# Expert mixture on one core: one row per token that experts gather, add to and scatter back, in place of three slots and a gather per group

## The chip, the cores and the metric

The kernel runs on one core of a Trainium2 chip. The metric is device time in microseconds of one execution; lower is better.

## What is computed

A trunk layer with two parts. The first mixes tokens: 2048 tokens and 16 meta tokens of width 1024 are normalised, projected by `w_in`, run through gated linear attention and latent attention, and projected back by `w_out`. The second is a hierarchical mixture of experts: a token chooses one of 8 groups and in it 2 of 8 experts; each expert is a SwiGLU of width 512. The sum of the residual row and the two weighted expert outputs is normalised at the end.

```python
h = h + concat([y_gla, y_mla]) @ w_out
t = rmsnorm(h, ffn_norm)
g_p, g_idx = top_k(softmax(t @ wg + bg), 1)                 # one of 8 groups
e_p, e_idx = top_k(softmax(e_logits_of_group), 2)           # two of its 8 experts
gates = g_p * e_p / sum(e_p)
ys = (silu(xb @ w_gate[e]) * (xb @ w_up[e])) @ w_down[e]    # per expert, its tokens
h = h + scatter_add(ys * gate)
out = rmsnorm(h, final_norm)[16:]
```

## The kernel before, in words

The program is recorded by a scheduling framework. Tiles are taken from pools with a number of buffers; the framework sets the order of the earlier phases on each engine, and the expert phase follows an order that a planner (`moe_plan`, L1475) works out from costs and due times. Every operation of the expert phase is recorded through one helper, so in the trace they all stand at L124 and are told apart by their tiles.

**Start.** `phase_z` (L149) loads tiles of x by SP (`load_x`, L162, DMA at L164), squares them on ACT (L170), normalises them on DVE (L173), and loads `w_in` in twelve pieces `wraw` of 128 x 1024 by ACT's queue (`load_w`, L177, DMA at L179). Each piece is split into two parts that a matmul in fp32r takes: `wh`, a cast on ACT (L182), and `wl`, a subtraction on DVE (L183). Every matmul of full precision is thus three.

**Rows in DRAM.** `out_proj` (L1157) writes the residual rows h into slot 0 of `yd`, a DRAM tensor of 2048 rows of 3 x 1024 floats (L1170), and the normalised rows into `ud`. Slots 1 and 2 are zeroed by `clear` (called at L985, defined at L993, DMA at L995): 32 writes of 512 KB on SP's queue. They depend on nothing but a small tile of zeros.

**Routing.** `route` (L1006), `odds` (L1080) and `weights` (L1100) work out group, experts, ranks and gates per pair of token tiles, and build tables: `src`, the token in each of 112 places of each expert's block, gate and scale columns of `tab`, and `gtab`, the tokens of each group, in up to 384 places.

**Experts.** `phase_moe` (L1598) runs one block of 112 places per expert, experts 0 to 63 in their order. Weights come in raw pieces of 1 MB, three per expert (`Weight`, L1348, SP's queue, 5 buffers `raw`), which ACT casts to `hi` and DVE subtracts to `lo`; of the down projection a half is used raw. The steps of a block, by the planner's names: GA gathers the block's rows of `ud` into `xs` (POOL, an indirect DMA); TX, XH, XL turn and split them; M_g and M_u are the gate and up matmuls into `pg`; SILU is on ACT; PROD on DVE (`h<-pg,tab,sg`); TH, HH, HL, HC turn and split `h`; M_d are the down matmuls into `pd`; Y multiplies `pd` by the gate on ACT (`weigh`, L1674, two halves of 112x512); SC scatters `y` into slot 1 or 2 of its token in `yd` (L1688, POOL).

After each eight experts, a group is complete. GF (`collect`, L1698) gathers its rows, three tiles `fo` of 128 rows of 12 KB, from `yd` by the table `g_dst`; A adds the three slots on DVE (L1702); SQ squares with a sum on ACT (L1707); RS and R take a logarithm and an exponential for the root (L1712), with loads of activation tables; L scales on DVE (`finish`, L1719); OD scatters the finished rows to the output (L1722, POOL). These steps lie among those of the next group's blocks; those of the last group come after the last matmul. Experts or groups with more tokens than places are handled behind the loop by code that does not run with these inputs.

Of the kernel before, what the change touches and what calls it, by code (L numbers as in the profile page):

```python
# [8 lines left out]
F32 = mybir.dt.float32  # L9
F32R = mybir.dt.float32r  # L10
# [39 lines left out]
YB = 3  # L50
# [25 lines left out]
def build(tc, a, dbg=None, stop=99):  # L76
    nc = tc.nc
    dbg = dbg or {}
    with ExitStack() as top:
# [7 lines left out]
        yd = dram.tile([SEQ, 3, D], F32, name="yd")  # L87
# [12 lines left out]
        env = dict(tc=tc, nc=nc, a=a, dbg=dbg, zf=zf, zv=zv, qd=qd, qrd=qrd, hg=hg, ud=ud, yd=yd, xlist=xlist, xexp=xexp,  # L100
# [657 lines left out]
def phase_mix(tc, nc, a, qd, qrd, hg, ud, yd, xlist, xexp, kv, ident, ones, eps, rt, keep, ctx, right, g_rest, g_close, **_):  # L758
# [10 lines left out]
    gpos = keep.tile([P, NT], F32, name="gpos")  # L769
    rt.update(gix=gix_, gpos=gpos, iob=iob, ids=ids, rank=rank, gates=gates, eix=eix, rstd=rstd)  # L770
    with ExitStack() as out:
# [196 lines left out]
        def finish(H):  # L968
# [15 lines left out]
            if H.h % 2:  # L984
                clear(2 * H.i + H.h // 2)  # L985
# [4 lines left out]
        zero = keep.tile([P, 1, D // 8], F32, name="zero")  # L990
        nc.gpsimd.memset(zero, 0.0)
# [14 lines left out]
        def route(lg, j):  # L1006
# [17 lines left out]
            nc.gpsimd.tensor_copy(Es[:, :, NE:], goh)  # L1024
            nc.vector.tensor_mul(Es[:, :, :NE].rearrange("p t (g j) -> p t g j", j=8), ohs[:, :, None, :].to_broadcast([P, 2, 8, 8]), gohb)
# [24 lines left out]
            for k in range(2):  # L1050
                nc.vector.tensor_mul(pr[:, k], E[:, k], ps[:, :, :NE])
# [28 lines left out]
        def odds(v, goh, oh, el, ps, js):  # L1080
# [12 lines left out]
            prg = O.so.tile([P, 2, 8], F32, name="prg", bufs=1)  # L1093
            nc.vector.tensor_mul(prg, goh, ps[:, :, NE:])
            gp1 = gpos[:, js]
            nc.vector.tensor_reduce(gp1, prg, axis=AX.X, op=OP.add)
            nc.vector.tensor_scalar_add(gp1, gp1, 1.0)
            return gd, e2

        def weights(gd, e2, goh, oh, E, R, js, last):  # L1100
            gp1 = gpos[:, js]
# [8 lines left out]
            yield  # L1110
            R2 = O.so.tile([P, 2, 2, BS], F32, name="R2", bufs=1)
            nc.scalar.copy(R2, R)
            V2 = O.so.tile([P, 2, 2, 2, NE], F32, name="V2", bufs=1)
            for k in range(2):
                for c, q in ((1, rstd[:, js]), (0, gates[:, k, js])):
                    (nc.vector if last else nc.gpsimd).tensor_mul(V2[:, k, :, c], E[:, k], q[:, :, None].to_broadcast([P, 2, NE]))
            yield
            pool, tag = O.w0 if last else O.w
            pb = pool.tile([BS, 2, NE], F32, name="ptab", tag=tag)
            for k in range(2):  # L1120
                for t in range(2):
                    nc.tensor.matmul(pb, R2[:, k, t], V2[:, k, t], start=k + t == 0, stop=k + t == 2)
            nc.vector.tensor_add(tab[:, 2:4], tab[:, 2:4], pb)
            yield
            V = O.so.tile([P, 2, 3, 8], BF16, name="Vg", bufs=1)
            for c in range(2):
                nc.vector.tensor_mul(V[:, :, c], goh, tv[:, c, js, None].to_broadcast([P, 2, 8]))
            nc.vector.tensor_copy(V[:, :, 2], goh)
            pool, tag = O.h0 if last else O.w
            gt = pool.tile([24, GB], F32, name="gt", tag=tag)  # L1130
            for t in range(2):
                R = O.so.tile([P, GB], BF16, name="Rg", tag="Rg", bufs=1)
                nc.vector.tensor_scalar(R, it, gp1[:, t:t + 1], None, op0=OP.is_equal)
                nc.tensor.matmul(gt, V[:, t].rearrange("p c g -> p (c g)"), R, start=t == 0, stop=t == 1)
            nc.vector.tensor_add(gtab, gtab, gt)
            yield
            w8 = O.so.tile([P, 3, 2, 8], F32, name="w8", bufs=1)
            i8 = O.iota8.to_broadcast([P, 2, 8])
            nc.gpsimd.tensor_mul(w8[:, 2], goh, i8)
            for k in range(2):  # L1140
                nc.gpsimd.tensor_mul(w8[:, k], oh[:, k], i8)
            ix = O.so.tile([P, 3, 2], F32, name="ix", bufs=1)
            nc.vector.tensor_reduce(ix, w8, axis=AX.X, op=OP.add)
            nc.gpsimd.tensor_copy(gix_[:, js], ix[:, 2])
            for k in range(2):
                nc.vector.scalar_tensor_tensor(eix[:, k, js], ix[:, 2], 8.0, ix[:, k], op0=OP.mult, op1=OP.add)
# [10 lines left out]
        def out_proj(i, xs, yh, yl, hs, t, hf):  # L1157
# [11 lines left out]
            if hf and hs[-1] == 3:  # L1169
                nc.sync.dma_start(yd[j * P:j * P + P, 0], x)  # L1170
# [208 lines left out]
def extra_blocks(nc, sp, ps, rt, ones, fl, xlist, xexp):  # L1379
# [12 lines left out]
    nc.gpsimd.iota(lim, pattern=[[BS, NXE]], base=0, channel_multiplier=0, allow_small_or_imprecise_dtypes=True)  # L1392
# [25 lines left out]
    nc.gpsimd.iota(xo, pattern=[[0, 2]], base=0, channel_multiplier=BS, allow_small_or_imprecise_dtypes=True)  # L1418
# [15 lines left out]
def make_index(nc, sp, tab, src, first, rows, n):  # L1434
    s = sp.tile([rows, n], F32, name="mi_s", tag="mi_s", bufs=1)
    nc.vector.tensor_scalar(s, tab, float(SEQ), -float(SEQ), op0=OP.is_ge, op1=OP.mult)
    nc.vector.tensor_add(src, s, tab)
    nc.vector.tensor_scalar(first, tab, float(SEQ), None, op0=OP.is_lt)


def slot_index(nc, sp, dix, src, first, rows, n):
    s = sp.tile([rows, n], F32, name="si_s", tag="si_s", bufs=1)
    nc.vector.tensor_scalar(s, src, 3.0, 2.0, op0=OP.mult, op1=OP.add)
    nc.vector.tensor_sub(dix, s, first)


def group_table(nc, sp, ps, p_t, rt, ident):
# [13 lines left out]
    yield  # L1461
    gT = p_t.tile([P, GT, 24], F32, name="gT", tag="t")
    for c in range(GT):
        nc.tensor.transpose(gT[:, c], rt["gtab"][:, c * P:c * P + P], ident[:24, :24])
    tok = sp.tile([P, GT, 8], F32, name="g_tok", bufs=1)
    nc.vector.tensor_scalar(tok, gT[:, :, 16:24], -float(FAR), float(FAR), op0=OP.mult, op1=OP.add)
    for c in range(2):
        nc.vector.tensor_add(tok, tok, gT[:, :, 8 * c:8 * c + 8])
    nc.vector.tensor_scalar_mul(fg, fl, float(FAR))
    dst = sp.tile([P, GT, 8], I32, name="g_dst", bufs=1)  # L1470
    nc.vector.tensor_tensor(dst, tok, fg[:, None, :].to_broadcast([P, GT, 8]), op=OP.add)
    rt.update(fl=fl, goh=goh, dst=dst)
# [463 lines left out]
```

## Time and profile before

| | us |
|---|---|
| median of 3 runs | 2576.59 (2574.45 to 2579.51) |
| the profiled execution | 2573.4 |
| its span in the trace | 2571.7 |
| PE busy in the span | 2384.5 (93%) |
| DVE busy | 1703.2 (66%) |
| ACT busy | 1363.4 (53%) |
| POOL busy | 517.2 (20%) |

The span is cut into stages by time. Busy times of an engine overlap those of the others. The DMA share is the mean busy share of the core's 16 DMA engines, PEclk the clock that was granted to PE, as a part of full speed. A bracket at the end of a line of the timeline says how long the engine stood idle before the instruction and what released it.

### The profile page before, as it was taken

Reading aid. Unit: us, or ns where it says so; the run is one execution under the profiler, and the core shown is the slowest. Engines: PE = TensorE matmul, PEld = TensorE weight load, DVE = VectorE, ACT = ScalarE, POOL = GpSimd, SP = SyncE. Lnnn points to the kernel's source line nnn. Section 1 sums busy time; section 2 is a strip of 40 time slices with the busy share of each in tenths; the row PEclk is TensorE's granted clock in tenths of the full one; section 3 lists DMA queues with packets and bytes.
Section 4 is the critical chain, followed back from the end, with each engine's and each line's share of the span. In section 5 each row is a group of like instructions: output and inputs, shape, how many; then the busy total and the mean of one; then the engine's idle time right before and its main releaser. Section 6 shows DMA issues by size and latency. Waiting matters only on the chain. (4 is left out here: it accounts for less than half of the span.)

```text
span 2571.7 us, 35285 instructions
## 1 busy us (share of the span) xinstructions
PE 2384.5 (93%) x12900; PEld 1892.3 (74%) x12900; DVE 1703.2 (66%) x2684; ACT 1363.4 (53%) x2101; POOL 517.2 (20%) x550
## 2 busy tenths in 40 slices
PE   3899999799999999999699989999999999999993
PEld 3799999678788989989567656666666667667662
DVE  2534243577667676777777767777777777777773
ACT  2312111555346555555366666675766767766672
POOL 0000000542000111212421223222122322223221
PEclk7899999899999999999799999999999999999997
DMA  9512112555331221220699999999999999999993
GB/s 307 187 53 78 62 52 85 161 188 173 131 130 46 77 80 63 69 72 34 242 323 377 370 338 364 375 372 376 366 378 379 373 368 375 370 364 378 368 375 132
DMA packets 184959, 605.19 MB, mean 235 GB/s; under 512 B 28172, under 2 KB 103452, under 8 KB 133580
## 3 DMA queue, kind: packets, MB, share of 16 engines
q1 hardware_dynamic: 158892, 526.49, 56.2%
q0 software_dynamic: 23440, 67.68, 7.1%
q10 hardware_dynamic: 2448, 8.72, 1.0%
q8 instruction: 103, 1.69, 0.3%
q14 instruction: 76, 0.62, 0.1%
HBM read 538.10 MB, written 106.63 MB: 251 GB/s over the span
## 5 line engine op out<-in xcount | busy, mean ns | idle before, releaser
L124 DVE TENSOR_TENSOR lo<-raw,hi 128x2048 fp32r<-128x2048 f32 x317 | 719.9, 2287 | 196.3 <-ACT hi L124 191.9
L124 ACT CAST hi<-raw 128x2048 fp32r<-128x2048 f32 x318 | 605.9, 1908 | 374.0 <-DMA raw<-in_w_gate_dram 207.9
L124 PE MATMUL pg<-hi,xh 128*112 128x512 f32 x1024 | 436.7, 426 | 0.9 <-ACT xh L124 0.9
L124 PE MATMUL pg<-lo,xh 128*112 128x512 f32 x1024 | 405.3, 396 | 16.7 <-DVE lo L124 16.7
L124 PE MATMUL pg<-hi,xl 128*112 128x512 f32 x1024 | 411.0, 401 | 9.2 <-DVE xl L124 9.2
L135 PE MATMUL ps<-uh,wh 128*128 128x256 f32 (+2 forms) x768 | 223.8, 292 | 31.9 <-ACT wh L182 20.8
L124 PEld LDWEIGHTS pg<-lo,xh 128*112 128x112 f32 x1024 | 181.6, 177 | 89.0 <-DVE lo L124 19.9
L124 PEld LDWEIGHTS pg<-hi,xl 128*112 128x112 f32 x1024 | 180.4, 176 | 72.1 <-DVE xl L124 13.3
L124 PEld LDWEIGHTS pg<-hi,xh 128*112 128x112 f32 x1024 | 180.3, 176 | 68.7 <-issue 9.6
L124 PE MATMUL pd<-raw,hc 128*112 128x512 f32 x512 | 230.1, 592 | 0.0
L137 PE MATMUL ps<-uh,wl 128*128 128x256 f32 (+3 forms) x768 | 222.1, 289 | 1.5 <-DVE wl L183 1.5
L136 PE MATMUL ps<-ul,wh 128*128 128x256 f32 (+2 forms) x768 | 222.8, 290 | 0.2 <-DVE ul L224 0.2
L124 POOL DMA_INDIRECT yd<-y,dix x64 | 135.5, 2118 | 408.3 <-ACT y L124 408.3
L124 POOL DMA_INDIRECT xs<-ud,src x64 | 100.4, 1569 | 432.4 <-PE pt L124 413.8
L135 PEld LDWEIGHTS ps<-uh,wh 128*128 128x128 f32 (+1 forms) x768 | 149.2, 194 | 33.9 <-ACT wh L182 22.2
L124 PEld LDWEIGHTS pd<-raw,hc 128*112 128x112 f32 x512 | 90.4, 177 | 104.4 <-issue 97.0
L137 PEld LDWEIGHTS ps<-uh,wl 128*128 128x128 f32 (+1 forms) x768 | 149.0, 194 | 2.8 <-DVE wl L183 2.5
L136 PEld LDWEIGHTS ps<-ul,wh 128*128 128x128 f32 (+1 forms) x768 | 149.4, 195 | 0.9 <-DVE ul L224 0.5
L124 PE MATMUL pd<-hi,hh 128*112 128x512 f32 x256 | 110.0, 430 | 18.1 <-ACT hh L124 18.1
L257 DVE COPY st<-ps 128x256 f32<-128x256 f32 (+1 forms) x64 | 27.0, 422 | 145.4 <-PE ps L137 145.3
L124 PE MATMUL pd<-hi,hl 128*112 128x512 f32 x256 | 105.4, 412 | 2.0 <-DVE hl L124 1.8
L124 PE MATMUL pd<-lo,hh 128*112 128x512 f32 x256 | 104.9, 410 | 0.0
(2430 smaller groups left out, 5047.2 us busy)
## 6 DMA issues: line engine op xcount, KB each, us to landing
raw<-in_w_gate_dram SPq DMA_DIRECT2D x128, 1024.0 KB
raw<-in_w_up_dram SPq DMA_DIRECT2D x128, 1024.0 KB
raw<-in_w_down_dram SPq DMA_DIRECT2D x128, 1024.0 KB
x<-in_x_dram SPq DMA_DIRECT2D x32, 512.0 KB
yd<-zero SPq DMA_DIRECT2D x32, 512.0 KB
zf<-st SPq DMA_DIRECT2D x85, 128.0 KB
hg<-x SPq DMA_DIRECT2D x16, 512.0 KB
x<-hg SPq DMA_DIRECT2D x16, 512.0 KB
```

What stands on the lines that cost most here:

```text
L124: return self.tc.keep_in_program_order(f(*args, **kw))
L135: nc.tensor.matmul(out, lh, rh, start=start, stop=False, **kw)
L136: nc.tensor.matmul(out, lh, rl, start=False, stop=False, **kw)
L137: nc.tensor.matmul(out, ll, rh, start=False, stop=stop, **kw)
L257: nc.vector.tensor_copy(st[:w, :n - o], ps[:w, :n - o])
```

## The change

`yd` becomes `hz`, one row of 1024 floats per token, which holds h. The writes of zeros are gone. Experts are taken as e = 8 (i mod 8) + i // 8: the first expert of each group, then the second of each, and so on, so a token's two experts lie at least eight blocks apart. The gate is multiplied into PROD's scale (`grs`). Each block now gathers the rows of its tokens from `hz` (GB, tile `b`), adds the expert's output to them on DVE (Y, tile `z`), and scatters the sum back to `hz` for tokens whose other expert is still to come (SZ, `t_zd`; the other places point out of bounds and are left out). Every block also takes the square (SQ, on ACT), the root by an addition and a power on POOL (RT), scales (L, on DVE), and scatters the rows of tokens that are complete to the output (SO, `t_od`). No gather per group is left. Dependences between rows of different groups are declared away (`apart`). `RAWB` goes from 5 to 6 raw buffers; `xh` and `xl` move to another pool; the routing loses the group table and gains the flag of which expert of a token is first.

```diff
-WC = 72
-GB = 384
-GT = GB // P
-RAWB = 5
+WC = NE
+RAWB = 6
...
-YB = 3
+ZB = 3
+BB = 2
+OB = 2
...
-        yd = dram.tile([SEQ, 3, D], F32, name="yd")
+        hz = dram.tile([SEQ, D], F32, name="hz")
...
-            if H.h % 2:
-                clear(2 * H.i + H.h // 2)
...
-        def clear(t):
-            for k in range(2):
-                nc.sync.dma_start(yd[t * P:t * P + P, 1 + k].rearrange("t (a d) -> t a d", a=8), zero.to_broadcast([P, 8, D // 8]))
...
+            f = O.so.tile([P, 2, 2], F32, name="f", bufs=1)
+            for k in range(2):
+                nc.vector.tensor_tensor(f[:, k], ix[:, k], ix[:, 1 - k], op=OP.is_lt)
+            Ef = O.so.tile([P, 4, NE], BF16, name="Ef", bufs=1)
...
+            for k in range(2):
+                for t in range(2):
+                    nc.tensor.matmul(pb[:, 0], R[:, k, t], Ef[:, 2 * k + t], start=k + t == 0, stop=k + t == 2)
+            nc.vector.tensor_add(tab[:, 1:4], tab[:, 1:4], pb)
...
-                nc.sync.dma_start(yd[j * P:j * P + P, 0], x)
+                nc.sync.dma_start(hz[j * P:j * P + P], x)
...
-        op(f"Y{j}", -1, "A", 0.62, (("M_d1a", "M_d1")[j], 0), ("Y0", 0) if j else ("SD", YB))
+        op(f"Y{j}", -1, "V", 0.7, (("M_d1a", "M_d1")[j], 0), ("Y0", 0) if j else ("BQ", 0), *([] if j else [("L", ZB), ("ZQ", ZB)]))
...
-    op("SC", -1, "G", 2.1, ("Y1", 0))
-    op("SD", -1, "Q", 4.5, ("SC", 0))
-    for c in range(GT):
-        op(f"GF{c}", -2, "G", 2.1, ("SD", 1), (f"OD{c}", 8), *([(f"GF{c - 1}", 0)] if c else []))
...
+    op("GB", -1, "G", 1.7, ("Y1", BB), ("ZQ", 8))
+    op("BQ", -1, "Q", 5.0, ("GB", 0))
+    op("SZ", -1, "G", 2.1, ("Y1", 0))
+    op("ZQ", -1, "Q", 5.0, ("SZ", 0))
+    op("SQ", -1, "A", 1.3, ("Y1", 0), ("OQ", OB))
+    op("RT", -1, "G", 0.3, ("SQ", 0))
+    op("L", -1, "V", 1.3, ("RT", 0))
+    op("SO", -1, "G", 2.1, ("L", 0))
+    op("OQ", -1, "Q", 5.0, ("SO", 0))
...
+    for e in range(0, NE + 1):
+        for n, d in (("SZ", 2.5), ("SQ", 6.0), ("L", 9.0), ("SO", 10.0)):
+            if (n, e) in nodes:
+                late[n, e] = late["M_d1", e] + W + d
...
-            S.xh = rp.tile([P, KD, BS], F32R, name="xh", tag="xh", bufs=1)
-            S.xl = rp.tile([P, KD, BS], F32R, name="xl", tag="xl", bufs=1)
+            S.xh = pools.sp.tile([P, KD, BS], F32R, name="xh", tag="xh", bufs=1)
+            S.xl = pools.sp.tile([P, KD, BS], F32R, name="xl", tag="xl", bufs=1)
...
-        on.scalar.mul(S.y[:, cs], S.d[hf], S.gate)
...
+    def apart(o, S, old):
+        for q, g in old:
+            if g != S.e // 8:
+                tc.declare_no_dep(o.ins, q.ins, reason="rows of tokens of other groups")
+
+    def base(S):
+        S.b = sp.tile([BS, D], F32, name="b", tag="b", bufs=BB)
+        o = gather(S.b, S.src, hz)
+        apart(o, S, rows.put)
+        rows.got.append((o, S.e // 8))
+
+    def plus(S, hf):
...
+        on.vector.tensor_add(S.z[:, cs], S.d[hf], S.b[:, cs])
+
+    def keep_z(S):
+        o = spread(hz, rt["zd"][:, S.e:S.e + 1], S.z)
...
+    def square(S):
...
+        on.scalar.activation(S.o, S.z, AF.Square, scale=D ** -0.5, accum_out=S.ss)
...
+    def root(ss):
+        on.gpsimd.tensor_scalar(ss, ss, EPS, None, op0=OP.add)
+        on.gpsimd.tensor_tensor(ss, ss, half[:ss.shape[0]], op=OP.pow)
+
+    def last_norm(S):
+        on.vector.scalar_tensor_tensor(S.o, S.z, S.ss, rows.gain[:BS], op0=OP.mult, op1=OP.mult)
+
+    def leave(S):
+        o = spread(out, rt["od"][:, S.e:S.e + 1], S.o)
...
-    B = [block(xsb[e % XSB], wg[e], wu[e], wd[e], tab[:, 2, e:e + 1], tab[:, 3, e:e + 1], rt["src"][:, e:e + 1], e) for e in range(NE)]
+    grs = sp.tile([BS, NE], F32, name="grs", bufs=1)
+    B = [block(xsb[i % XSB], wg[e], wu[e], wd[e], grs[:, e:e + 1], tab[:, 3, e:e + 1], rt["src"][:, e:e + 1], e, i)
+         for i, e in enumerate(8 * (i % 8) + i // 8 for i in range(NE))]
```

The order of the instructions, at the three places that matter. On SP, from its first instruction, before (`zero` is the tile of zeros):

```order
L164 DMA x<-in_x_dram 128x1024 x2
L164 DMA x<-in_meta_tokens_dram 16x1024
L995 DMA yd<-zero 128x8x128 x11
L164 DMA x<-in_x_dram 128x1024
L995 DMA yd<-zero 128x8x128 x8
L164 DMA x<-in_x_dram 128x1024
L995 DMA yd<-zero 128x8x128 x10
```

and after:

```order
L164 DMA x<-in_x_dram 128x1024 x2
L164 DMA x<-in_meta_tokens_dram 16x1024
L164 DMA x<-in_x_dram 128x1024 x3
L259 DMA zf_57<-st 128x256
L259 DMA zf_58<-st 128x256
```

The writes of zeros, which stood between the loads of x, are gone, and the loads stand together.

On POOL, in the middle of the expert phase, around the end of a group before:

```order
L124 DMA xs_13946<-ud,src 112x1024
L124 DMA yd<-y,dix 6144x1024
L124 DMA fo<-yd,g_dst 128x3072 x2
L124 DMA xs_13762<-ud,src 112x1024
L124 DMA yd<-y,dix 6144x1024
L124 DMA xs_13944<-ud,src 112x1024
L124 DMA fo<-yd,g_dst 128x3072
L124 DMA yd<-y,dix 6144x1024
```

and one block after:

```order
L124 DMA hz<-z,t_zd 2048x1024
L124 DMA b<-hz,src 112x1024
L124 TENSOR_SCALAR ss<-ss 112x1
L124 TENSOR_TENSOR ss<-ss,half 112x1
L124 DMA out_dram<-o,t_od 2048x1024
L124 DMA xs_13831<-ud,src 112x1024
```

Every block now has two scatters, two gathers and the two operations of the root, in this row; before it had a scatter and a gather, and now and then one of a group.

On DVE, one block before:

```order
L124 TENSOR_TENSOR lo_15854<-raw,hi 128x2048
L124 TENSOR_TENSOR lo_15874<-raw,hi 128x2048
L124 TENSOR_TENSOR lo_15897<-raw,hi 128x2048
L124 TENSOR_TENSOR hl<-pth,hh 128x224
L124 TENSOR_TENSOR lo_15918<-raw,hi 128x2048
L124 TENSOR_TENSOR lo_15957<-raw,hi 128x2048
L124 SCALAR_TENSOR_TENSOR h<-pg,tab,sg 112x128x4
```

and after:

```order
L124 TENSOR_TENSOR z<-pd,b 112x512
L124 TENSOR_TENSOR xl<-pt,xh 128x448
L124 TENSOR_TENSOR lo_15374<-raw,hi 128x2048
L124 TENSOR_TENSOR z<-pd,b 112x512
L124 TENSOR_TENSOR lo_15395<-raw,hi 128x2048
L124 TENSOR_TENSOR lo_15410<-raw,hi 128x2048
L124 SCALAR_TENSOR_TENSOR o<-z,ss,gain 112x1024
L124 TENSOR_TENSOR hl<-pth,hh 128x224
L124 TENSOR_TENSOR lo_15455<-raw,hi 128x2048
L124 TENSOR_TENSOR lo_15489<-raw,hi 128x2048
L124 SCALAR_TENSOR_TENSOR h<-pg,grs,sg 112x128x4
```

Two `z` and the scaling `o` have come in, the latter between two `lo` and `hl`.

## Rows read from the trace of the kernel before

**Rows 1.** Windows by stage; columns: us, busy (count) per engine, PEclk, DMA share, GB/s.

```profile
0.00:120.00 120.00, 68.15 (x393) 60.95 (x394) 47.49 (x58) 36.88 (x66) 2.73 (x16) 0.79 0.85 261
120.00:330.00 210.00, 210.00 (x1551) 200.02 (x1550) 72.27 (x108) 33.23 (x72) 0.00 (x0) 1.00 0.18 63
330.00:1240.00 910.00, 875.58 (x5777) 772.70 (x5776) 606.72 (x1789) 440.02 (x1107) 170.04 (x337) 0.98 0.31 103
...
1306.37:2506.44 1200.07, 1159.45 (x4883) 808.78 (x4881) 906.08 (x613) 810.09 (x803) 306.17 (x160) 0.98 0.98 371
2531.41:2571.70 40.29, 0.01 (x1) 0.00 (x0) 10.94 (x9) 5.62 (x13) 7.75 (x7) 0.54 0.34 132
```

**Rows 2.** Timeline of SP: first and last of the zero writes.

```profile
3.05 20.80 SPq L995 DMA_DIRECT2D yd<-zero  x11
...
62.71 5.69 SPq L995 DMA_DIRECT2D yd<-zero  x3
```

**Rows 3.** Timeline of ACT at the start: casts and issues of w_z.

```profile
13.87 1.04 ACT L182 CAST wh<-wraw 128x1024 fp32r<-128x1024 f32 x1
...
67.05 1.04 ACT L182 CAST wh<-wraw 128x1024 fp32r<-128x1024 f32 x1 [24.50 <-DMA yd<-zero]
...
81.48 0.34 ACTq L179 DMA_DIRECT2D wraw<-in_w_z_dram  x1
...
82.62 0.33 ACTq L179 DMA_DIRECT2D wraw<-in_w_z_dram  x1
...
88.63 0.33 ACTq L179 DMA_DIRECT2D wraw<-in_w_z_dram  x1
...
99.95 0.34 ACTq L179 DMA_DIRECT2D wraw<-in_w_z_dram  x1
```

**Rows 4.** Timeline of DVE: the first normalised tile of x.

```profile
7.88 1.28 DVE L173 SCALAR_TENSOR_TENSOR x<-x,rstd,gain 128x1024 f32<-128x1024 f32 x1 [6.66 <-ACT rstd L146]
```

**Rows 5.** Windows: eight blocks before group work; gather of xs, scatter, group gather.

```profile
1343.66:1492.66 149.00, 146.26 (x633) 103.38 (x632) 109.42 (x73) 95.95 (x91) 33.04 (x18) 1.00 0.96 377
...
1822.00:1825.00 3.00, 3.00 (x13) 1.97 (x12) 3.00 (x3) 3.00 (x5) 0.00 (x0) 1.00 1.02 258
1830.00:1834.00 4.00, 4.00 (x19) 3.01 (x18) 1.46 (x3) 2.15 (x2) 0.00 (x0) 1.00 1.02 425
1775.00:1785.00 10.00, 10.00 (x41) 6.39 (x39) 5.66 (x6) 5.67 (x6) 2.52 (x3) 1.00 1.01 417
```

**Rows 6.** Timeline of POOL: issues of indirect transfers.

```profile
1771.12 1.04 POOL L124 DMA_INDIRECT fo<-yd,g_dst  x1 [7.72 <-DMA yd<-y,dix]
1772.46 3.10 POOL L124 DMA_INDIRECT fo<-yd,g_dst  x1 [0.30 <-issue]
...
1817.01 1.39 POOL L124 DMA_INDIRECT xs<-ud,src  x1 [7.11 <-PE pt L124]
```

**Rows 7.** Groups by form, 1340 to 2500: busy, mean ns of one | idle before.

```profile
L124 DVE TENSOR_TENSOR lo<-raw,hi 128x2048 fp32r<-128x2048 f32 x295 | 669.9, 2287 | 183.9 <-ACT hi L124 181.7 <-issue 1.0
...
L124 ACT ACTIVATE y<-pd,tab 112x512 f32<-112x512 f32 x118 | 78.4, 691 | 11.0 <-PE pd L124 10.6
...
L124 DVE SCALAR_TENSOR_TENSOR fo<-fo,fss,gain 128x1024 f32<-128x1024 f32 x20 | 25.6, 1278 | 0.0
L124 ACT ACTIVATE fo<-fo 128x1024 f32<-128x1024 f32 x21 | 22.3, 1063 | 0.0
```

**Rows 8.** Groups of DVE, 1100 to 1240: an add from PSUM of 128x512.

```profile
L1163 DVE TENSOR_TENSOR x<-x,psh 128x512 f32<-128x512 f32 x16 | 10.8, 685 | 12.5 <-PE psh L137 12.3
```

**Rows 9.** Groups of POOL, 330 to 1240: a small operation.

```profile
L1144 POOL COPY gix<-ix 128x2 f32<-128x2 f32 x7 | 1.8, 263 | 0.0
```

**Rows 10.** Window at the start of the expert phase, columns as in rows 1.

```profile
1245.00:1250.00 5.00, 0.33 (x3) 0.18 (x3) 4.83 (x14) 0.00 (x0) 3.75 (x9) 0.75 0.13 52
```

**Rows 11.** Timeline of POOL at the end: first and last scatter to the output.

```profile
2555.03 1.80 POOL L124 DMA_INDIRECT out_dram<-fo,g_dst  x1 [14.63 <-DVE fo L124]
...
2558.44 0.97 POOL L124 DMA_INDIRECT out_dram<-fo,g_dst  x1 [0.30 <-issue]
```

More of the change, by code (lines that the diff above doesn't have):

```diff
@@ L1065, in route @@
                     for c in range(2):
-                        nc.tensor.matmul(pi[:, 0], R[:, k, t], V1[:, c, k, t], start=k + t + c == 0, stop=k + t + c == 3)
-            for t in range(2):
-                nc.tensor.matmul(pi[:, 1], R[:, 0, t], E[:, 0, t], start=t == 0, stop=t == 1)
+                        nc.tensor.matmul(pi, R[:, k, t], V1[:, c, k, t], start=k + t + c == 0, stop=k + t + c == 3)
             if last:
-                nc.vector.tensor_add(rt["src"], tab[:, 0], pi[:, 0])
-                o = nc.vector.tensor_add(rt["first"], tab[:, 1], pi[:, 1])
+                o = nc.vector.tensor_add(rt["src"], tab[:, 0], pi)
                 with tc.issue_after(o.ins):
@@ L1110, in weights @@
             yield
+            eng = nc.vector if last else nc.gpsimd
+            w8 = O.so.tile([P, 3, 2, 8], F32, name="w8", bufs=1)
+            i8 = O.iota8.to_broadcast([P, 2, 8])
+            eng.tensor_mul(w8[:, 2], goh, i8)
+            for k in range(2):
+                eng.tensor_mul(w8[:, k], oh[:, k], i8)
+            ix = O.so.tile([P, 3, 2], F32, name="ix", bufs=1)
+            nc.vector.tensor_reduce(ix, w8, axis=AX.X, op=OP.add)
+            eng.tensor_copy(gix_[:, js], ix[:, 2])
+            for k in range(2):
+                nc.vector.scalar_tensor_tensor(eix[:, k, js], ix[:, 2], 8.0, ix[:, k], op0=OP.mult, op1=OP.add)
+            yield
+            f = O.so.tile([P, 2, 2], F32, name="f", bufs=1)
+            for k in range(2):
+                nc.vector.tensor_tensor(f[:, k], ix[:, k], ix[:, 1 - k], op=OP.is_lt)
+            Ef = O.so.tile([P, 4, NE], BF16, name="Ef", bufs=1)
+            nc.vector.tensor_mul(Ef, E.rearrange("p k t j -> p (k t) j"), f.rearrange("p k t -> p (k t)")[:, :, None].to_broadcast([P, 4, NE]))
             R2 = O.so.tile([P, 2, 2, BS], F32, name="R2", bufs=1)
@@ L1120, in weights @@
             for k in range(2):
                 for t in range(2):
[L1122 to L1137, printed above, removed]
@@ L1138, in weights @@
-            i8 = O.iota8.to_broadcast([P, 2, 8])
-            nc.gpsimd.tensor_mul(w8[:, 2], goh, i8)
-            for k in range(2):
[L1141 to L1146, printed above, removed]
+                    nc.tensor.matmul(pb[:, 1:3], R2[:, k, t], V2[:, k, t], start=k + t == 0, stop=k + t == 2)
@@ L1431, in extra_blocks, with flags @@
     rt["nxi"] = nxi
[L1434 to L1447, printed above, removed]
+def flags(nc, sp, ps, rt):
     cb = ps.tile([P, WC], F32, name="cb", tag="d")
@@ L1460, in group_table, with targets @@
     nc.vector.tensor_tensor(goh, gi.to_broadcast([P, NT, 8]), rt["gix"][:, :, None].to_broadcast([P, NT, 8]), op=OP.is_equal)
-    yield
-    gT = p_t.tile([P, GT, 24], F32, name="gT", tag="t")
-    for c in range(GT):
[L1464 to L1472, printed above, removed]
+    rt.update(fl=fl, goh=goh)
+def targets(nc, sp, rt):
+    tab, fl = rt["tab"], rt["fl"]
+    first = sp.tile([BS, 8, 8], F32, name="t_first", bufs=1)
+    nc.vector.tensor_max(first, tab[:, 1].rearrange("s (g j) -> s g j", j=8), fl[:BS, :, None].to_broadcast([BS, 8, 8]))
+    first = first.rearrange("s g j -> s (g j)")
+    zd = rt["zd"] = sp.tile([BS, NE], I32, name="t_zd", bufs=1)
+    od = rt["od"] = sp.tile([BS, NE], I32, name="t_od", bufs=1)
+    nc.vector.scalar_tensor_tensor(od, first, float(FAR), rt["src"], op0=OP.mult, op1=OP.add)
+    nc.vector.tensor_scalar(first, first, -float(FAR), float(FAR), op0=OP.mult, op1=OP.add)
+    nc.vector.tensor_add(zd, first, rt["src"])
 def moe_plan():
@@ L1594, in moe_plan, with phase_moe @@
     line.sort(key=lambda x: x[0])
-    return [(n, e, e + ops[n][0], nodes[n, e][0]) for _, (n, e) in line if n not in ("GD", "SD") and n[:2] != "GQ"]
-def phase_moe(tc, nc, a, ctx, ud, yd, xlist, xexp, ident, ones, eps, rt, out, **_):
+    return [(n, e, e + ops[n][0], nodes[n, e][0]) for _, (n, e) in line if n not in ("GD", "BQ", "ZQ", "OQ")]
+def phase_moe(tc, nc, a, ctx, ud, hz, xlist, xexp, ident, ones, eps, rt, out, **_):
     rp = rt["rp"]
@@ L1688, in scatter @@
-    def scatter(S):
-        o = put(S, rt["dix"][:, S.e:S.e + 1])
-        for q in rows.put + rows.got:
-            tc.declare_no_dep(o.ins, q.ins, reason="slots of other tokens")
-        rows.put.append(o)
-    def fetch(t, ix):
-        return on.gpsimd.indirect_dma_start(out=t.rearrange("p s d -> p (s d)"), out_offset=None, in_=yd.rearrange("t s d -> t (s d)"),
-                                            in_offset=bass.IndirectOffsetOnAxis(ap=ix, axis=0), bounds_check=SEQ - 1, oob_is_err=False)
@@ new lines, in keep_z @@
+    def keep_z(S):
+        o = spread(hz, rt["zd"][:, S.e:S.e + 1], S.z)
+        apart(o, S, rows.put + rows.got)
+        rows.put.append((o, S.e // 8))
+    def square(S):
+        S.o = sp.tile([BS, D], F32, name="o", tag="o", bufs=OB)
+        S.ss = sp.tile([BS, 1], F32, name="ss", tag="ss", bufs=4)
+        on.scalar.activation(S.o, S.z, AF.Square, scale=D ** -0.5, accum_out=S.ss)
+    half = sp.tile([P, 1], F32, name="half", bufs=1)
+    nc.vector.memset(half, -0.5)
+    def root(ss):
+        on.gpsimd.tensor_scalar(ss, ss, EPS, None, op0=OP.add)
+        on.gpsimd.tensor_tensor(ss, ss, half[:ss.shape[0]], op=OP.pow)
@@ L1749, in lo @@
     def lo(S, t, eng):
[L1750 removed]
+        made[S.e, t].low(pools, len(TILES) * (S.i + (t[0] == "d")) + TILES.index(t), eng)
     def use(S, t):
@@ L1770, in phase_moe @@
             do["M_" + t] = lambda S, g, t=t: proj(S, int(t[0] == "u"), int(t[1]), use(S, t))
-    for n, f, m in (("TX", flip, 2), ("XH", xhi, 2), ("XL", xlo, 2), ("Y", weigh, 2), ("GF", collect, GT), ("A", add, GT),
-                    ("SQ", square, GT), ("L", finish, GT), ("OD", leave, GT)):
-        for j in range(m):
+    for n, f in (("TX", flip), ("XH", xhi), ("XL", xlo), ("Y", plus)):
+        for j in range(2):
             do[f"{n}{j}"] = lambda S, g, f=f, j=j: f(S, j)
-    for c in range(GT):
-        do[f"R{c}"] = lambda S, g, c=c: root(S, slice(c, c + 1))
     eng = {"T": on.tensor, "V": on.vector, "A": on.scalar, "G": on.gpsimd}
     def tables():
-        rt["dix"] = sp.tile([BS, NE], I32, name="dix", bufs=1)
-        slot_index(nc, sp, rt["dix"], rt["src"], rt["first"], BS, NE)
-        yield from group_table(nc, sp, p_d, p_t, rt, ident)
-        rows.dst, fl = rt["dst"], rt["fl"]
-        yield from extra_blocks(nc, sp, p_d, rt, ones, fl, xlist, xexp)
-    for c in range(GT):
-        on.gpsimd.memset(sp.tile([P, 3, D], F32, name="fo", tag="fo", bufs=GT), 0.0)
+        nc.vector.tensor_mul(grs, tab[:, 2], tab[:, 3])
+        flags(nc, sp, p_d, rt)
+        yield
+        targets(nc, sp, rt)
+        yield
+        yield from extra_blocks(nc, sp, p_d, rt, ones, rt["fl"], xlist, xexp)
+    for _ in range(BB):
+        on.gpsimd.memset(sp.tile([BS, D], F32, name="b", tag="b", bufs=BB), 0.0)
     table = tables()
     for n, e, b, k in moe_plan():
-        if (n, b) == ("SC", 0):
+        if (n, b) == ("SZ", 0):
             gain = rows.gain = sp.tile([P, D], F32, name="gain", bufs=1)
@@ L1854, in phase_moe @@
             for hf in range(2):
-                weigh(S, hf)
-            put(S, di)
+                plus(S, hf)
+            spread(hz, S.src, S.z)
         ft = sp.tile([P, NT, 8], F32, name="xft", tag="xft", bufs=1)
```

154 lines of the change are left out of this document (46 added, 108 removed).

## Prediction

> **What bounds the kernel now.** I read the windows by stage first, then the queue that loads data at the start, then one window of the expert stage against another, then the end. [rows 1] cut the span of 2571.7 us. [...] In the expert stage, 1200.07 us from the first block's start to the 62nd's, PE is busy 97%, but the DMA share is 0.98: 61 blocks of 19.67 us, each with 19.3 us of DMA. DVE (906.08) and ACT (810.09) are far from that. After the last matmul 40.29 us follow in which PE does nothing.
>
> Who holds the start is shown by SP's queue [rows 2]: 32 writes of zeros of 512 KB, 16.8 MB in all, are issued from 3.05 to 68.4 us. ACT casts a piece of w_z at 13.87 and waits 24.50 us for the piece that it casts at 67.05; the trace names the zeros [rows 3].
>
> **Start: the zeros go.** Without them SP has the six x loads at its head and no write of zeros. [...] After the zeros, the last six of the twelve pieces of w_z are issued from 81.48 to 99.95, 3.7 us apart [rows 3]; at that pace, with the second cast free at about 16 us and nine pieces to come, the last is issued at 16 + 9 x 3.7 = 49 us, 51 earlier than now. With the longest gap among them throughout (82.62 to 88.63, 6.0 us) it is 70, 30 earlier. I take -46: nearer to the mean pace, since the long gaps stand beside short ones, less some us because the x loads, which the zeros held back, now come at the same time. Bounds -30 and -55.
>
> **Experts: bytes per block.** A block has some 64 of 112 rows in use (4096 token-expert pairs over 64 experts), 0.26 MB. Before: a gather of 0.26, a scatter of 0.26, per block an eighth of the group's gather of 256 rows of 12 KB (0.39 MB), and 0.13 out. After: the same gather, one more gather from hz of 0.26 (GB), and scatters of half the rows each to hz and to out, together 0.26. So a block of the changed kernel is a block without group work plus GB. Eight such blocks stand in the trace before the first group ends: 149.00 us, 18.63 each, DMA share 0.96, so 17.9 us of DMA each [rows 5].
>
> No row shows GB. Its nearest row is the gather of the same shape from ud: in the 3 us behind its issue at 1817.01 [rows 6] the rate is 258 GB/s against 377 of the eight blocks, with all queues full (share 1.02); behind scatters (425) and in the group's gather of 12-KB rows (417) it is not lower at all [rows 5]. Over 3 to 4 us that loses 3 x (1 - 258/377) = 0.9 to 1.3 us, and its own 0.26 MB are 0.7: 1.6 to 2.0. At the bytes alone, at 417 GB/s, it is 0.6. I take 1.6, the low end of the nearest row, because the same POOL queue will issue GB apart from the other gather. 17.9 + 1.6 = 19.5 of DMA, at a share of 0.98 to 1 a block of 19.5 to 19.9. I take 19.7: 61 x 0.03 = **+2**. Bounds: at 0.6 DMA needs 18.5, PE 146.26 / 8 = 18.3, and a block would stand near 18.9 (-47); at 2.0 it is 20.2 (+32).
>
> [...]
>
> **Engines beside it.** ACT loses two Y of 0.691 and gains a square of 1.063 [rows 7]: nothing. DVE gains two z, as the 128x512 add from PSUM, 0.685 each [rows 8], and one L, 1.278 [rows 7]: 109.42 / 8 = 13.7 [rows 5] + 2.65 = 16.3 of 19.7 us. It stays under the DMA, so 0, with a wait as a rival below. POOL gets two more transfers and two small operations a block, about 0.26 each as the nearest one [rows 9]; four issues of 1 to 3.1 us [rows 6] and these fill at most 13 of 19.7 us: 0. Routing drops the group table and adds flags and four small matmuls: 0, within 2 us, beside matmuls that fill the stretch. The table loads that go are on ACT, which has time.
>
> **Expert start.** The sixth raw buffer lets one more megabyte of weights be fetched where the DMA stands nearly idle (0.13 in 1245 to 1250 [rows 10]): 1 MB at 377 GB/s is 2.8, **-3**, or 0 where that stretch is held by something else.
>
> **End.** Now 40.29 us: scatter, its landing, three group gathers, adds, norms, and three scatters to out, of which the last is issued by 2558.44 + 0.97, 12.3 us before the end [rows 11]. After: z 0.7, square 1.1, root 0.5, L 1.3, issue 1.8 as the first of the three [rows 11], landing 12.3: 17.7, so **-22.5**. Bounds -20 (an issue of 3.1 and slow small operations) and -26 (one scatter lands sooner than three).
>
> **Sum**: -46 + 2 - 3 - 22.5 = -69.5 on the profiled execution's 2573.4 (span 2571.7 and 1.7 around it), 2503.9. The median shown, 2576.59, is 3.2 above that execution, so I predict **2507**. Its own band, with the start and the gather at their middle values, is 2485 to 2530.
>
> **Rivals.** *First, the gather is cheap*, 0.6 us: blocks of 18.9, bound by PE and DMA alike. For: bytes fall from 1.04 to 0.78 MB a block beside the weights, and the gathers of 12-KB rows cost only their bytes. Against: 258 GB/s for the same shape. Time: -46 - 3 - 47 - 22.5 = -118.5, so 2458. Chance 0.2.
>
> *Second, slower: POOL's row.* In the new order POOL issues the scatter to hz and the gather from hz ahead of the two operations of the root, and DVE has L ahead of hl, which the down projection needs, and of two lo. The square cannot start before both z, and two lo of 2.287 [rows 7] are all that DVE does between the second z and L. If the two issues take 3.1 each [rows 6] rather than 1.4, 6.2 + 0.5 after z stand against 4.6 of cover: 2 us of waiting a block, if DVE has not run ahead. It decides from (46 + 3 + 22.5) / 61 = 1.2 us a block, blocks over 20.8; with 2 us, 61 x 2 - 71.5 = +50, 2627. For: the same issue took 1.04 and 3.10 us. Against: DVE has 3.4 us a block to spare, and PE runs on weights prepared ahead. Chance 0.07.
>
> [...]
>
> *Third, the start gives little*: the pieces of w_z wait because ACT, which issues them itself, waits for x and PSUM, and the zeros only came last. For: ACT's queue mixes issues, casts and squares. Against: the waits of 24.50 us end with the zeros. If only the one wait of 24.50 is won, less 4 us of new sharing, -20: -20 + 2 - 3 - 22.5 = -43.5, 2533. Chance 0.1.
>
> **How the numbers follow.** Forecast 0.55, rivals 0.2, 0.07 and 0.1, and 0.08 for a mixture (a dear gather at +32 with a small start, -30, would still be 2573.4 - 23.5 + 3.2 = 2553). The range reaches over the third rival and most of the first: 2450 to 2548. A measurement of this kernel tells about 0.2%, 5 us, from no change. Faster 0.91: forecast, first, third and nearly all of the mixture; same 0.02, slower 0.07.
>
> **What would show it.** Right: PE's 393rd matmul near 74 us rather than 120, and no wait of ACT over 10 us there; blocks of 19.7 with a DMA share of 0.98 and dips to 260 GB/s twice a block; some 18 us behind the last matmul. First rival: blocks under 19.1. Second: hl or L waiting for POOL, DMA share under 0.95. Third: the same waits of ACT at 27 to 67 us, released by x or w_z. Above 2553 or below 2445 the working is wrong in its largest terms.

## The result, and the profile after

| | before | changed |
|---|---|---|
| median, us | 2577.93 (4 runs) | 2516.64 (2515.02 to 2518.82, 4 runs) |
| ratio | | 0.9765 (0.9748 to 0.9782) |
| span of the profiled execution | 2571.7 | 2515.7 |

The change takes 61 us off; 2507 was predicted. The windows by stage of the changed kernel, with the columns of [rows 1]; the experts' stage again runs from the first block's start to the 62nd's, and the last window begins 0.27 us before the last matmul ends:

```profile
0.00:120.00 120.00, 106.05 (x738) 96.50 (x739) 63.36 (x82) 44.40 (x82) 1.62 (x11) 1.00 0.46 146
120.00:330.00 210.00, 210.00 (x1576) 201.77 (x1576) 74.68 (x112) 32.45 (x71) 0.00 (x0) 1.00 0.18 62
...
1251.28:2473.15 1221.87, 1165.07 (x4883) 802.34 (x4881) 978.32 (x731) 760.00 (x732) 609.73 (x363) 0.99 0.98 353
2473.15:2500.00 26.85, 25.08 (x98) 15.89 (x96) 17.37 (x17) 9.63 (x12) 12.71 (x9) 1.00 0.35 130
2500.00:2515.70 15.70, 0.27 (x1) 0.00 (x0) 1.98 (x2) 1.15 (x2) 2.79 (x4) 0.63 0.13 39
```

Beside [rows 1] the reader is to see: 738 matmuls in the first 120 us where 393 stood, at a granted clock of 1.00 where it was 0.79; an experts' stage that is 21.8 us longer (1200.07 before), with the same DMA share of 0.98 at 353 GB/s where it was 371; and 15.4 us behind the last matmul for 40.29. The stages give the whole: the experts start 55.1 us earlier (1306.37 to 1251.28), their 61 blocks take 21.8 more, the last two blocks 2.2 more, the end some 24.9 less: -56.0, the difference of the spans.

At the start, ACT's queue. The issues of the third, the tenth and the twelfth piece of w_z, of which the last six stood at 81.48 to 99.95 in [rows 3]:

```profile
14.88 0.33 ACTq L179 DMA_DIRECT2D wraw<-in_w_z_dram  x1
...
40.20 0.34 ACTq L179 DMA_DIRECT2D wraw<-in_w_z_dram  x1
...
48.38 0.34 ACTq L179 DMA_DIRECT2D wraw<-in_w_z_dram  x1
```

The twelfth piece is issued at 48.38; 49 was worked out from the pace of 3.7 us.

In the experts' stage, groups by form from 1290 to 2400, with the columns of [rows 7]:

```profile
L124 PE MATMUL pg<-hi,xl 128*112 128x512 f32 x887 | 360.0, 406 | 44.3 <-DVE xl L124 44.3
...
L124 POOL DMA_INDIRECT hz<-z,t_zd x56 | 171.7, 3066 | 408.3 <-DVE z L124 408.3
...
L124 PE MATMUL pd<-hi,hl 128*112 128x512 f32 x220 | 88.5, 402 | 6.3 <-DVE hl L124 6.1
L124 DVE SCALAR_TENSOR_TENSOR o<-z,ss,gain 112x1024 f32<-112x1024 f32 x55 | 70.7, 1285 | 98.0 <-POOL ss L124 98.0
```

The wait of the second rival is there: L (`o<-z,ss,gain`) waits 98.0 / 55 = 1.8 us a block for POOL's root, and PE waits for `xl` and a little for `hl` behind it. So two causes stood for the 21.8 us: the DMA time of the second gather, or POOL's row of issues. The experiments tell them apart.

### The profile page after: what moved, and what is told of

It is laid out like the page before. It is cut to its first block, busy times and chain, and to the rows that moved or that the text cites. A ratio compares the mean times of both kernels' runs of the same rounds, so it can differ in the third digit from the quotient of the medians.

```text
span 2515.7 us, 35600 instructions
## 1 busy us (share of the span) xinstructions
PE 2371.7 (94%) x12897; PEld 1876.6 (75%) x12897; DVE 1761.5 (70%) x2756; ACT 1307.3 (52%) x2018; POOL 816.6 (32%) x740
## 5 line engine op out<-in xcount | busy, mean ns | idle before, releaser
L124 POOL DMA_INDIRECT hz<-z,t_zd x64 | 195.1, 3049 | 463.1 <-DVE z L124 454.4
L135 PE MATMUL ps<-uh,wh 128*128 128x256 f32 (+3 forms) x768 | 219.1, 286 | 0.7 <-ACT uh L223 0.7
L136 PE MATMUL ps<-ul,wh 128*128 128x256 f32 (+3 forms) x768 | 218.8, 285 | 0.0
L124 DVE SCALAR_TENSOR_TENSOR o<-z,ss,gain 112x1024 f32<-112x1024 f32 x64 | 82.2, 1285 | 118.5 <-POOL ss L124 118.5
L124 POOL DMA_INDIRECT out_dram<-o,t_od x64 | 121.3, 1895 | 105.0 <-DVE hl L124 88.8
L124 POOL DMA_INDIRECT xs<-ud,src x64 | 136.3, 2130 | 44.6 <-PE pt L124 22.3
```

The costliest lines, as they stand in the source:

```text
L124: return self.tc.keep_in_program_order(f(*args, **kw))
L135: nc.tensor.matmul(out, lh, rh, start=start, stop=False, **kw)
L136: nc.tensor.matmul(out, lh, rl, start=False, stop=False, **kw)
```

## The experiments

Blocks are the time from the first block's start to the 62nd's over 61, in the one execution that was profiled; the times are medians. Every time stands beside runs of the kernel before on the same chip, whose median was 2578 to 2579.

| run | us | a block, us | DMA share, GB/s |
|---|---|---|---|
| changed kernel | 2516.6 | 20.03 | 0.98, 353 |
| zeros_back | 2563.8 | 20.08 | 0.98, 352 |
| b_out_of_bounds | 2448.8 | 19.05 | 0.96, 358 |
| b_none | 2438.0 | 18.58 | 0.94, 368 |
| l_late | 2521.7 | 20.06 | 0.99, 352 |
| raw5 | 2527.9 | 20.21 | 0.97, 351 |
| b_plain | 2530.1 | 20.25 | 0.99, 350 |
| one_gather6 | 2532.9 | 20.05 | 0.98, 353 |
| spread | 2509.3 | 19.79 | 0.98, 357 |
| shuffled | 2536.9 | 20.26 | 0.98, 349 |
| before_spread | 2574.3 | 19.73 | 0.98, 371 |
| one_gather_spread | 2522.7 | 19.92 | 0.98, 356 |
| aligned | 2430.3 | 18.58 | 0.98, 381 |

**zeros_back** puts the zero writes back into the changed kernel.

```diff
+        zy = dram.tile([SEQ, 2, D], F32, name="zy")
...
+            if H.h % 2:
+                clear(2 * H.i + H.h // 2)
```

> The changed kernel with the 32 zero writes put back at the same place of the source, to a scratch tensor that nobody reads. If the start's gain is the zeros' doing (last piece of w_z cast at 51.3 us in place of 103.0): the cast of the last piece returns to 100 to 105 us and the time rises by 48 to 55, to 2565 to 2572. If the start is shorter because the scheduler orders it otherwise without yd: a rise under 15.

The first two windows and the experts' stage of this kernel:

```profile
0.00:120.00 120.00, 66.99 (x390) 60.24 (x391) 47.55 (x58) 36.89 (x66) 1.77 (x12) 0.79 0.87 261
120.00:330.00 210.00, 210.00 (x1549) 199.76 (x1547) 71.73 (x108) 33.14 (x72) 0.00 (x0) 1.00 0.19 63
1305.61:2530.27 1224.66, 1165.53 (x4883) 803.44 (x4881) 980.19 (x731) 762.02 (x732) 606.43 (x363) 0.99 0.98 352
```

The start of before is back: 390 matmuls, clock 0.79. The last piece of w_z is cast at 103.78, the experts start 54.3 us later than in the changed kernel, and the median rises by 47, 1 us short of what was expected; the profiled execution is the slowest of six (2558 to 2572). So the start's gain is the zeros', and the third rival falls. How large it is is known to some 6 us: the runs below that differ from the changed kernel only in the experts' blocks start these at 1253.96 to 1257.23, the changed kernel itself at 1251.28. All else that the change does ahead of the experts (sixth raw buffer, smaller routing) shows as 1306.37 - 1305.61 = 0.8 us, which is below that.

**b_out_of_bounds** and **b_none** take the bytes, or all, of the second gather away; both leave out of the result what the gather would bring. The edit of b_out_of_bounds (in b_none, `S.b` is one tile of zeros):

```diff
-        o = gather(S.b, S.src, hz)
+        o = gather(S.b, rt["none"][:, S.e:S.e + 1], hz)
```

> The gather from hz keeps its place and its issue on POOL, but all its indices lie out of bounds, so it moves no row; the block adds what lies in b instead of h (that part of the result is left out). If the experts' blocks of 20.03 us are bound by the DMA time of the second gather: blocks of 18.7 to 19.1, 57 to 80 us less, 2437 to 2460, DMA share under 0.97. If POOL's row of issues and the wait of L for the root hold the blocks: 19.7 to 20.1 still, 2495 to 2520, and L waits for POOL as before.

> The gather from hz is left out altogether, with its issue; b is zero (that part of the result is left out). DMA theory: as with all indices out of bounds, within 8 us of it, 2437 to 2460. POOL theory: one issue of 1.7 us less in each block's row, so L's mean wait of 1.8 us nearly gone: blocks near 19, 2455, and well below the run with indices out of bounds.

The experts' stage of b_none:

```profile
1253.96:2387.16 1133.20, 1133.20 (x4883) 800.25 (x4881) 982.61 (x733) 760.20 (x732) 588.92 (x302) 1.00 0.94 368
```

and L in b_out_of_bounds, groups by form from 1290 to 2400:

```profile
L124 DVE SCALAR_TENSOR_TENSOR o<-z,ss,gain 112x1024 f32<-112x1024 f32 x58 | 74.5, 1285 | 182.6 <-POOL ss L124 182.6
```

Without the gather PE is never idle, 18.58 a block. With its issue kept and its rows gone, L waits longer than ever, 3.1 us a block, and yet a block takes 19.05. That is the slower of two executions, 2464.4 and 2433.2, which lie 31 us apart, 0.5 us a block; the faster one stands where b_none does. So the rows that the gather moves cost 1.0 us a block or more, and whether its issue on POOL costs anything, 0.5 at most, is open; that b_none came 11 us under b_out_of_bounds where 8 was the bound lies inside that spread. The DMA time a block is 20.03 x 0.98 = 19.6 with the gather and 18.58 x 0.94 = 17.5 without, so the gather costs 2.1 us of it. By queue, its own packets are 0.84 of this; the other 1.23 are the packets of the weights, which take longer beside it.

**l_late** moves L behind `hl` on DVE.

```diff
-        for n, d in (("SZ", 2.5), ("SQ", 6.0), ("L", 9.0), ("SO", 10.0)):
+        for n, d in (("SZ", 2.5), ("SQ", 6.0), ("L", 14.0), ("SO", 15.0)):
```

> Only the due time of L and of the last scatter in the planner goes from 9 and 10 to 14 and 15, so that L stands behind hl and a third lo on DVE. DMA theory: L's wait for POOL (107 us over the stage) shrinks to under 30, the blocks stay at 19.9 to 20.1 and the time within 6 us of 2516.6. POOL theory: PE's waits for xl and hl (46.4 and 6.9 us over the stage) go with it, 20 to 50 us less, 2465 to 2497.

Groups by form of l_late, the same stretch:

```profile
L124 PE MATMUL pg<-hi,xl 128*112 128x512 f32 x881 | 359.6, 408 | 19.7 <-DVE xl L124 19.0
L124 POOL DMA_INDIRECT hz<-z,t_zd x55 | 286.4, 5208 | 332.7 <-DVE z L124 332.7
...
L124 DVE SCALAR_TENSOR_TENSOR o<-z,ss,gain 112x1024 f32<-112x1024 f32 x55 | 70.7, 1285 | 81.4 <-POOL ss L124 81.4
```

PE's waits for `xl` more than halve, those for `hl` are gone, and the block stays at 20.06, at a DMA share of 0.99: what PE gains there it waits for elsewhere. The detail of the expectation is missed: L's wait did not go under 30, because the scatter's issue on POOL grew from 3.07 to 5.21 us (on this, the last section).

**raw5** goes back to five raw buffers.

> The changed kernel with five raw buffers in place of six, as before the change. If the sixth buffer is worth what the prediction said: 3 us more at the start of the experts, no more in their blocks. If the prefetch of one more piece carries the blocks over the slow stretches of the gathers: blocks of 20.3 or more, 20 us or more on the time.

Two runs, 2521.9 and 2533.9; 20.21 us a block in the profile, which is of the slower one, between the two expectations. The experts start at 1257.70, half a us later than in b_out_of_bounds, which has six buffers. What the sixth buffer is worth, and where, two runs 12 us apart do not settle.

**b_plain** and **one_gather6** ask what makes the gather dear. In b_plain the block adds rows of other tokens, so that part of the result is left out.

```diff
-        o = gather(S.b, S.src, hz)
+        r = 64 * (S.i % 32)
+        on.gpsimd.dma_start(S.b[:64], ud[r:r + 64])
```

> The gather from hz is replaced by an ordinary transfer of 64 neighbouring rows of ud from the same queue: the same bytes in rows of 4 KB, but no indices (the block adds rows of other tokens; that part of the result is left out). If the gather costs what its bytes in 4-KB rows cost the DMA engines: blocks of 19.6 to 20.1. If it is the indirect form (indices, rows left out, scattered rows) that costs: blocks of 18.6 to 19.1, 55 to 85 us less than the changed kernel.

```diff
-        ud = dram.tile([SEQ, D], F32, name="ud")
-        hz = dram.tile([SEQ, D], F32, name="hz")
+        uh = dram.tile([SEQ, 2, D], F32, name="uh")
...
-    op("GA", 2, "G", 2.1, ("TX1", 0))
+    op("GA", 2, "G", 2.1, ("TX1", 0), ("Y1", 1), ("ZQ", 5))
...
+    def base(S):
+        o = gather(S.xs, S.src)
```

> A version that is meant to be better: u and h of a token lie side by side in one row of 8 KB in DRAM, one gather per block, three blocks ahead, fetches both, the second gather and its issue are gone; the scatter goes to the second half of the row. The bytes of a block are those of the changed kernel. If bytes decide: blocks of 19.8 to 20.1 and 2505 to 2520. If the second gather costs by its form and its rows: blocks of 18.6 to 19.2, 2430 to 2470, PE bound (18.58 a block without the gather).

Both stay at 20 us a block and more, 20.25 and 20.05: it is not the indices, nor that the rows lie apart in DRAM, nor their 4 KB. (one_gather6 has the changed kernel's blocks; its further 16 us lie outside, the experts start at 1261.84.) By the expectations' letter this left the bytes; but the group gather of before moved its bytes at 417 GB/s [rows 5] (over all 21 issues, 404 in the 4 us that begin 6 us behind the start), and a theory of bytes does not explain that. What the slow transfers share is their partitions: 64, or 64 in use of 112, where the fast one had 128. (Of the packet times in the next expectation, 211 ns is a mean, 434 and 313 are medians; the weights' mean in one_gather6 was 354.)

**spread**, **shuffled**, **before_spread**, **one_gather_spread** deal the places of a block out to other partitions; `iob` is the table that says which rank a place takes.

```diff
-    nc.gpsimd.iota(iob, pattern=[[0, 1], [1, BS]], base=0, channel_multiplier=0, allow_small_or_imprecise_dtypes=True)
+    for c, step, n, first in ((0, 2, 48, 0), (48, 1, 16, 96), (64, 2, 48, 1)):
+        nc.gpsimd.iota(iob[:, :, c:c + n], pattern=[[0, 1], [step, n]], base=first, channel_multiplier=0, allow_small_or_imprecise_dtypes=True)
```

In shuffled the loop runs over `((0, 2, 32, 0), (32, 2, 32, 1), (64, 1, 48, 64))`.

> The changed kernel, but the places of a block are dealt out alternately to partitions 0 to 47 and 64 to 111 (48 to 63 last), so that 64 rows lie on 0 to 31 and 64 to 95 in place of 0 to 63. Bytes, rows, indices and instructions are the same. Theory: gathers are slow because their rows land on partitions 0 to 63 alone; the plain transfer to these (4 KB, 211 ns a packet) and the gather of 8-KB rows (434 ns, where weights take 313) were as slow. Then both gathers of a block get quick, the weights beside them too: blocks of 18.6 to 19.0, DMA share 0.97 or less, 2425 to 2460. [...] If the cost is in the rows (4 KB, scattered in DRAM) or in the indirect form: no change, 2510 to 2523.

> A control: the places are dealt out to even and odd partitions in turn, but the first 64 stay on partitions 0 to 63. Partition theory: no change from the changed kernel, 2510 to 2523, blocks of 19.9 to 20.2. If it is the neighbourhood of rows or the order of descriptors that matters: faster, as with alternate halves.

> The kernel before the change with the same alternate places. Partition theory: its one gather per block gets quick too, so the blocks outside the ends of groups, bound by PE at 18.63, stay, and those that waited after the group's gathers shrink: 19.67 to 19.0 to 19.4 a block, 15 to 40 us less, 2538 to 2562. Row theory: no change.

> The version with one gather of 8-KB rows, with the alternate places. Partition theory: its 64 rows of 8 KB get quick, blocks of 18.6 to 18.9, 2430 to 2455, and with one issue on POOL less at least as fast as the changed kernel with alternate places. Row theory: 2530 as before.

The theory of the halves falls: spread gains 7 us where 55 and more were expected (its 19.79 us a block are of the fastest of four executions), before_spread 5 (0.9974, 0.9957 to 0.9991) where 15 to 40 were, one_gather_spread 10 against one_gather6. The control is a miss too: it should not have moved, and lost 20. So the place of the rows does matter, but not as the theory of the halves has it.

**aligned** is spread with gathers of 128 places; nothing else differs. What speaks for it is the one row of this shape, the group gather of before: 128 partitions and 417 GB/s [rows 5], where all the slow transfers have 112 or 64. If the shape is what counts, the blocks shrink.

```diff
-        rt["src"] = keep.tile([BS, NE], I32, name="src")
+        rt["src"] = keep.tile([P, NE], I32, name="src")
+        nc.gpsimd.memset(rt["src"], SEQ)
...
-            t = rp.tile([BS, D], F32, name=f"xs{j}")
+            t = rp.tile([P, D], F32, name=f"xs{j}")
...
-        S.b = sp.tile([BS, D], F32, name="b", tag="b", bufs=BB)
+        S.b = sp.tile([P, D], F32, name="b", tag="b", bufs=BB)
```

> The version with alternate halves, and both gathers of a block are given 128 places in place of 112, the last 16 out of bounds: the same rows reach the same partitions. [...] Then blocks of 18.6 to 19.0, 2425 to 2460, the rate behind a gather at 400 and more. If it is the size of the rows, or 64 rows in use whatever the shape: no change from alternate halves, 19.7 to 19.9 a block, 2500 to 2515.

The experts' stage of aligned, and in it 4 us, some 4 to 8 us behind the issue of a gather from hz at 1611.80, in which its packets move:

```profile
1252.60:2385.79 1133.19, 1133.19 (x4882) 800.24 (x4881) 980.99 (x733) 753.72 (x732) 544.13 (x363) 1.00 0.98 381
...
1616.00:1620.00 4.00, 4.00 (x23) 3.21 (x23) 3.97 (x4) 3.31 (x5) 1.13 (x1) 1.00 0.97 395
```

and 4 us of the changed kernel, some 6 to 10 us behind such an issue at 1618.54:

```profile
1625.00:1629.00 4.00, 4.00 (x13) 1.92 (x11) 2.29 (x2) 2.44 (x3) 2.72 (x1) 1.00 0.83 246
```

These are two single windows, and not at the same distance. Over all such issues of the stage, the 4 us that begin 6 us behind the start of the issue have 293 GB/s in the changed kernel, 303 in spread and 378 in aligned. Compared with spread, the same rows land in the same partitions, and 16 places that fetch nothing are added to each gather: 19.79 becomes 18.58 a block (20.03 in the changed kernel), and PE is never idle. The time is 2430.33 us, 0.9435 (0.9412 to 0.9459) of the kernel before: this version beats both.

The same run decides on the second rival. L in aligned, groups by form from 1290 to 2400:

```profile
L124 DVE SCALAR_TENSOR_TENSOR o<-z,ss,gain 112x1024 f32<-112x1024 f32 x60 | 77.1, 1285 | 113.0 <-POOL ss L124 113.0
```

With all issues of POOL in place L still waits for the root, 113.0 / 60 = 1.9 us a block, as long as in the changed kernel, and PE waits for nothing.

Why the shape counts no run shows. The runs show that it does: 2430.3 us in aligned and 2509.3 in spread, and the weights' packets beside the gathers 331 and 355 ns on average (last section). Whether 128 places alone suffice, in the old order of places, was not tried.

## Why the prediction was right, and where it was off

- **Start, -46 (bounds -30 and -55).** Right in the mechanism; 54.3 in the profiles of zeros_back and the changed kernel. PE's 739th matmul starts 49.5 us earlier (120.05 against 169.52), so the "some us" kept back for x loads that now come at the same time were not there; the other 4.8 us come later, ahead of the experts, from what is not shown. The signs held: the 393rd matmul starts at 71.8 us, ACT's longest wait in the first 120 us is 9.8. The bound of -55 is an estimate: by [rows 1] 393 matmuls at 210.00 / 1551 = 0.135 us fill 53 of the first 120 us, 67 are left, and some 12 of them were kept for the first loads. No run shows the 12; PE's first matmul starts at 9.31 us before and at 9.15 in the changed kernel.
- **Experts' start, -3.** Not seen: -0.8 for all that remains when the zeros are back, in executions whose experts start up to 6 us apart. No run shows that the idle DMA at 1245 to 1250 [rows 10] became earlier work of PE.
- **Experts, +2.** Right that the DMA bounds the stage before and after, share 0.98, and right in what a gather costs: its own packets (0.84 us a block, 0.7 forecast) and the weights' beside it (1.23, 0.9 to 1.3 forecast). What is off is the size: "I take 1.6, the low end of the nearest row, because the same POOL queue will issue GB apart from the other gather". It measured 2.1, just above the upper end of 2.0; the weights' packets took 357 ns on average and 331 in b_none without GB, though POOL issues it 7 us ahead of the next gather from ud and 13 behind the one before it (medians). The block without it was off the other way, 17.5 us of DMA in b_none where 17.9 was taken from [rows 5]. So the sum of 19.5 came near the measured 19.6 by luck, and most of the distance from 19.7 a block to 20.03 is the share, 0.98 where 19.7 needs 0.99. The row of 258 GB/s was lucky too: it is one window, 5 to 8 us behind the issue and not the 3 us behind it, and over all 58 such gathers of the kernel before that stretch has 298, which would have made the price smaller.
- **Engines beside it, 0.** Right: l_late, b_none and aligned show that POOL's and DVE's waits cost the kernel nothing, behind the DMA in the changed kernel (20.06 us a block in l_late for 20.03, with PE's waits for `xl` at 19.7 us for 44.3) and behind PE in b_none and aligned (18.58, PE never idle).
- **End, -22.5.** Measured -24.9, with the last two blocks 2.2 slower: -22.7 together.
- **Sum.** -69.5 was forecast, -56.0 came between the profiled executions: the blocks were 19.8 us dearer than forecast and the experts' start 2.2, the start of the kernel 8.3 better, the end 0.2. The medians are 61.3 apart. That the median came within 10 us of the forecast is in part luck: a start better than forecast stands against dearer blocks.
- **First rival.** False as it was put, for this shape of gather; but aligned runs at the PE-bound block that it needed, 18.58 with both gathers in place. The 0.6 us that the prediction works out for GB's bytes at the 417 GB/s of [rows 5] are an estimate far off for a gather of 112 places, 2.1. They are not contradicted by one of 128: the DMA time is 18.58 x 0.976 = 18.1 us a block in aligned, 0.6 over b_none's 17.5, though in aligned both gathers have the new shape.
- **Second rival.** Its wait is real, 1.8 us a block, and did not decide: aligned has it too, and PE is never idle there. **Third rival**: refuted by zeros_back.

## What to carry to other kernels

Writes that nothing waits for, put on a queue at the very start, cost some 50 us here, beside the first loads: look for such writes where a short span shows a DMA share near 1 and an idle PE (before, the first 68 us had a share of 1.02, with PE busy for 23.46). Where the DMA bounds a stage, price an added transfer by the row of the same shape, with what it takes from its neighbours, and try the shape itself: with the traffic beside it, the stretch in which a gather of 112 places moves its rows ran at 303 GB/s on average, and at 378 when the same rows were fetched into the same partitions as one of 128. A long wait in the trace (L for POOL) is no cause until a run without it is faster.

## What the runs showed of the hardware that was not expected

First, the shape of a gather, above: on the DMA records of the trace, packets of 8 KB of the weights took 357 ns on average in the changed kernel, 355 in spread, and 331 in aligned, as in b_none without any second gather.

Second, POOL's issue of an indirect transfer waits for DVE. Timeline of POOL in the changed kernel:

```profile
1615.46 2.77 POOL L124 DMA_INDIRECT hz<-z,t_zd  x1 [5.28 <-DVE z L124]
...
1636.48 0.97 POOL L124 DMA_INDIRECT hz<-z,t_zd  x1 [8.76 <-DVE z L124]
...
1657.69 4.98 POOL L124 DMA_INDIRECT hz<-z,t_zd  x1 [9.09 <-DVE z L124]
```

and of DVE:

```profile
1615.10 2.28 DVE L124 TENSOR_TENSOR lo<-raw,hi 128x2048 fp32r<-128x2048 f32 x1
...
1636.52 2.29 DVE L124 TENSOR_TENSOR lo<-raw,hi 128x2048 fp32r<-128x2048 f32 x1 [0.32 <-ACT hi L124]
...
1657.32 4.48 DVE L124 TENSOR_TENSOR lo<-raw,hi 128x2048 fp32r<-128x2048 f32 x2
```

An issue that begins while DVE is idle takes 0.97 to 1.06 us; one that begins beside a `lo` ends about 0.97 after DVE's instruction ends (1615.10 + 2.28 + 0.97 = 1618.35, the issue ends at 1618.23), and beside two in a row it waits for both. Between 1300 and 2400 us 148 of 220 issues took over 1.3 us; all of these began while DVE was busy, and all ended 0.97 us, within 0.15, after the end of a `lo`, where 18% of moments taken at random lie so behind any instruction of DVE. Of the 36 issues that began while DVE was idle none took over 1.06. This is why l_late did not shorten L's wait as expected: without L between them more `lo` follow the second `z` at once, and the scatter's issue stands behind them (in l_late two `lo` run from 1655.91 to 1660.40, and the issue of 1656.28 ends at 1661.25). Why an issue waits for a `lo` no row shows.
